# Rank products issued behind each other, and products of zeros on TensorE at the start of a two-layer mixer kernel

## The chip, the core and the metric

The kernel runs on one core of a Trainium2 chip. The metric is the device time of one launch in microseconds (us). A core has a matrix engine (TensorE, called PE in the profile, with its weight loads as PEld), a vector engine (DVE), a scalar engine (ACT), GpSimd (POOL), and queues that issue DMA transfers, above all the one of SyncE (SP). Each engine works through its own list of instructions in the order in which the program has them. An instruction that waits holds up everything behind it on its engine.

## The reference, cut to what matters

Two layers work on 256 rows of `x` and 256 rows of a context `ctx`, both 2048 wide. The change touches only the beginning of layer 0: the modulation of both inputs, and the two narrow rank columns of the first projection.

```python
sh_c, sc_c = modulation(c_c, w_ada[i], b_ada[i], 2)      # silu(cond) @ w_ada + b_ada
sh, sc, gt = modulation(c_lat, w_ada[i], b_ada[i], 3)
u  = x     * (1.0 + sc)   + sh
uc = ctx_s * (1.0 + sc_c) + sh_c
# even mixer: k, v, rf, rb, q, ... = split_cols(u @ w_in_e, E_SIZES);  rf, rb are 16 columns each
la_f = log_sigmoid(rf @ w_gate_f + b_gate_f) / 16        # decays of the linear attention, forward
la_b = log_sigmoid(rb @ w_gate_b + b_gate_b) / 16        # and backward
...
x = layer_norm(alpha * x + gt * y, ln_g[i], ln_b[i])     # then layer 1, the pooling mixer
```

## The kernel before

All matrix products against weights are made in three parts: an input and a weight are each split into a high part (`uxh`, `wh`, a cast on ACT) and a remainder (`uxl`, `wl`, a subtraction on DVE), and `mm3` (L190 to L192) adds three products of them into a PSUM bank. Weights come as raw tiles of up to 1 MB through `load_unit` (L138) on the SP queue. There are four raw buffers: a load waits until the buffer's last reader is done, which is a split on DVE for the weights that are multiplied in three parts, and PE itself for the modulation weights `w_ada` of the beginning.

The first 180 us run over the 16 blocks of 128 input columns in nine stages (`STAGES`: one block, one block, then two at a time). `stage_u` makes the inputs of a stage. `mod_rows` multiplies `silu(c)` by `w_ada` into a PSUM tile `ada` (L274): these products use 32 of the array's 128 columns, and four of them, written to four strips of 32 PSUM rows, stand side by side in the array. `to_cols` brings the sum into columns (`adaT`, L288), `x` and `ctx` are transposed (`px`, L390 and L391), and ACT and DVE make the modulated inputs `u` and their high and low parts (L393 to L401). After every fourth block come the **rank products** (L406, tile `pr`): for each of the four blocks one product of its 32 rank columns `wr` with 512 rows of input, each into its own strip of 32 rows; DVE then adds `pr` into `r_acc` (L411, L413; the tile is called `wr_acc` in the rows). There are four such groups. Between the stages, `stage_k` makes the 1024 key columns of the stage before (`kacc`, summed into `knat` by DVE, L426), and `v_fill` makes a piece of the value columns in four of the stages (`vfill`).

From 180 us on the kernel makes the rest of the value columns, the gates, the attention, the output projection, and layer 1. Beside it DVE multiplies the remaining `w_ada` weights by scalars and sums them (`aacc`, L534).

The order on each engine is not written by hand: a scheduler sets it when the program is built, from the dependencies and from a priority number that grows with the place in the source. `prio(-n)` makes the instructions inside it count as n places earlier; `issue_after` ties an instruction behind another one. PSUM tiles come from two pools of four banks each: `accp` for the sums of the three-part products, `mpp` for everything else (`ada`, `px`, `pr` and so on).

Of the kernel before, what the change touches and what calls it, by code (L numbers as in the profile page):

```python
# [2 lines left out]

# [14 lines left out]
P = 128  # L18
# [21 lines left out]
LA_LOAD = 2  # L40
FILLS = {2: [(0, 0, 2)], 4: [(0, 2, 2)], 6: [(0, 4, 2)], 8: [(0, 6, 2)]}
FILL_PRIO = 0
SPLIT_PRIO = 300
SPLIT_PRIO0 = 0
XC_PRIO = 0
# [8 lines left out]
B_X = 3000  # L54
LA_SPLIT = 1
JG = 4
STAGES = (1, 1, 2, 2, 2, 2, 2, 2, 2)


@with_exitstack  # L60
def kernel(
# [39 lines left out]
    @contextmanager  # L101
    def prio(offset):
        old = tc.cur_priority
        tc.cur_priority = max(0, old + offset)
        start = tc.cur_priority
        yield
        tc.cur_priority = old + tc.cur_priority - start

    def const(shape, dt, name):
        return cpool.tile(shape, dt, tag=name, name=name)  # L110
# [4 lines left out]
    def mp(shape, name="mp"):  # L115
        return mpp.tile(shape, F32, tag="mp", name=nm(name))
# [108 lines left out]
    nc.gpsimd.dma_start(rows2[8:24, :], as_rows(pool_scale[0]))  # L225
    nc.gpsimd.dma_start(rows2[24:26, :], as_rows(gla_norm_w[0]))

    sel4 = const([P, 4], F32, "sel4")
    nc.vector.tensor_reduce(out=sel4, in_=ident.rearrange("p (g v) -> p v g", g=4)[:, 0:4, :], axis=AX.X, op=ALU.add)

# [1 line left out]
    nc.vector.memset(sil, 0.0)  # L232
    pc = mp([P, 32], "pc")
    nc.tensor.transpose(out=pc, in_=crow, identity=ident[:32, :32])
    nc.scalar.activation(sil[:, :, 2:4], pc.rearrange("p (v k) -> p k v", v=2), AF.Silu)

    colT = const([P, 154], F32, "colT")
# [25 lines left out]
    def mod_rows(k0, n):  # L263

        nw = n * P
        ps = mp([P, nw], "ada")
        nk = 2048 // nw
        for half, c0 in ((0, D + k0 * P), (1, k0 * P)):
            for kk in range(0, KT, nk):
                r = load_unit(w_ada[0], kk, nk, c0, nw)  # L270
                for j in range(nk):
                    kt = kk + j
                    g = kt % 4
                    nc.tensor.matmul(  # L274
                        out=ps[32 * g : 32 * g + 32, :], lhsT=sil[:, kt, 2 - 2 * half : 34 - 2 * half], rhs=r[:, j, :],
                        start=half == 0 and kt < 4, stop=half == 1 and kt >= KT - 4,
                    )
        return ps

    arow_ins = []  # L280
# [85 lines left out]
    def stage_u(k0, n):  # L366
        w, n0 = n * P, k0 * P
        xc = xcs.pop(k0, None)
        if xc is None:
            xc = load_xc(k0, n)  # L370
        xs, cs = xc[:, 0:2, :], xc[:, 2:4, :]
        ps = mod_rows(k0, n)
        if k0 == 0:
            cols_0()
        if k0 == 4:
            cols_1()
        if k0 == GW_AT:
            gate_weights()
        pt = to_cols(ps, w)
        ks = slice(k0, k0 + n)  # L380
        add_bias(scT[:, ks, :], pt[:, :, 0:2], bT[0][:, 16 + k0 : 16 + k0 + n].unsqueeze(2).to_broadcast([P, n, 2]), True)
        add_bias(shT[:, ks, :], pt[:, :, 2:4], bT[0][:, ks].unsqueeze(2).to_broadcast([P, n, 2]), False)
        for j in range(n):
            kt = k0 + j
            if kt % 2 == 0:
                quad_u.append(slot([P, 2, 512], F32, "u"))
            u = quad_u[-1]
            px = mp([P, 512], "px")
            for t in range(2):
                nc.tensor.transpose(out=px[:, t * P : (t + 1) * P], in_=xs[:, t, j * P : (j + 1) * P], identity=ident)  # L390
                nc.tensor.transpose(out=px[:, 256 + t * P : 256 + (t + 1) * P], in_=cs[:, t, j * P : (j + 1) * P], identity=ident)  # L391
            ux, uc = u[:, kt % 2, 0:256], u[:, kt % 2, 256:512]
            nc.scalar.activation(ux, px[:, 0:256], AF.Identity, bias=shT[:, kt, 0:1], scale=scT[:, kt, 0:1])  # L393
            nc.vector.tensor_scalar(
                out=uc, in0=px[:, 256:512], scalar1=scT[:, kt, 1:2], scalar2=shT[:, kt, 1:2], op0=ALU.mult, op1=ALU.add
            )
            q, i = kt // 4, kt % 4
            nc.scalar.copy(uxh[q][:, i, :], ux)  # L398
            nc.scalar.copy(uch[q][:, i, :], uc)
            nc.vector.tensor_tensor(out=uxl[q][:, i, :], in0=ux, in1=uxh[q][:, i, :].bitcast(F32), op=ALU.subtract)  # L400
            nc.vector.tensor_tensor(out=ucl[q][:, i, :], in0=uc, in1=uch[q][:, i, :].bitcast(F32), op=ALU.subtract)  # L401
            if i == 3:
                pr = mp([P, 512], "pr")
                for g in range(4):
                    kk = kt - 3 + g
                    nc.tensor.matmul(  # L406
                        out=pr[32 * g : 32 * g + 32, :], lhsT=wr[:, kk, :], rhs=quad_u[kk // 2][:, kk % 2, :],
                        start=True, stop=True,
                    )
                if q == 0:  # L410
                    nc.vector.tensor_copy(r_acc, pr)  # L411
                else:
                    nc.vector.tensor_tensor(out=r_acc, in0=pr, in1=r_acc, op=ALU.add)  # L413

    def stage_k(k0, n):
        for nb in range(2):
# [971 lines left out]
```

## Time and profile before

| what | us |
|---|---|
| median of three runs | 1009.52 |
| lowest and highest of them | 1008.19, 1010.95 |
| the profiled execution, its own time | 1010.29 |
| its span from the first to the last instruction | 1008.5 |
| PE busy in the span | 960.9 (95%) |
| DVE busy in the span | 801.6 (79%) |
| ACT busy in the span | 469.3 (47%) |

The span is 1.8 us shorter than the execution's own time. A busy share is read with care on PE: matmuls are pipelined, and their ends are modelled, so that records overlap. What tells the pace of PE is the distance from one start to the next. In the chain of work that ended last, PE has 41% of the span, DVE 33% and DMA 18%.

### The profile page before, as it was taken

The numbers are of one execution on the slowest core, as the hardware profiler recorded it, in microseconds if no ns is written. First come the engines' busy times: TensorE is split into PE (matmuls) and PEld (weight loads), VectorE is DVE, ScalarE is ACT, GpSimd is POOL, SyncE is SP. The second block draws the span as 40 slices with busy tenths as digits, with TensorE's granted clock in tenths as the row PEclk, the third lists the DMA queues.
The fourth block names the chain that finished last, engine by engine and source line by source line (L and its number), as shares of the span: only waits on it lengthen the run. The fifth ranks groups of instructions, "written<-read, shape, count | busy, mean of one in ns | idle before, by whom it ended". The sixth has DMA issues, their size and how long they took to land.

```text
span 1008.5 us, 14323 instructions
## 1 busy us (share of the span) xinstructions
PE 960.9 (95%) x5654; PEld 759.2 (75%) x5654; DVE 801.6 (79%) x1142; ACT 469.3 (47%) x643; POOL 24.4 (2%) x56
## 2 busy tenths in 40 slices
PE   5899999999999999999999899999999999989995
PEld 4566656778878877887878778888778778778885
DVE  1555546979996999779999688897979997666676
ACT  2422214356675676236454344445745555435340
POOL 2000000000000000000000000000010001000000
PEclk9999999999999999999999999999999999999998
DMA  9977889566787586867767877985497999875532
GB/s 265 329 263 262 276 284 336 193 243 231 258 302 252 188 269 219 257 206 274 241 228 234 284 255 247 353 298 207 152 368 275 304 334 322 278 266 203 174 119 83
DMA packets 150371, 255.44 MB, mean 253 GB/s; under 512 B 5078, under 2 KB 46720, under 8 KB 150304
## 3 DMA queue, kind: packets, MB, share of 16 engines
q1 hardware_dynamic: 146592, 245.13, 72.4%
q0 software_dynamic: 2896, 8.72, 2.7%
q10 hardware_dynamic: 816, 0.68, 0.3%
q8 instruction: 44, 0.72, 0.3%
q14 instruction: 23, 0.19, 0.0%
HBM read 252.41 MB, written 2.10 MB: 252 GB/s over the span
## 4 chain that ended last, share of the span: by engine, by line
PE 41%; DVE 33%; DMA 18%; issue 5%; ACT 3%; SPq 0%; DVEq 0%; ACTq 0%
DMA raw<-in_w_ada_dram 15%; DVE wl L153 11%; DVE aacc L534 9%; PE oacc L191 5%; PE oacc L192 5%; PE oacc L190 5%; DMA raw<-in_w_in_o_dram 3%; PE xacc L192 3%; PE xacc L191 3%; PE xacc L190 3%; PE ada L274 2%; PE kacc L190 2%; PE kacc L192 2%; PE kacc L191 2%; PE pr L406 1%
## 5 line engine op out<-in xcount | busy, mean ns | idle before, releaser
L152 ACT CAST wh<-raw 128x1024 fp32r<-128x1024 f32 (+1 forms) x250 | 257.0, 1044 | 252.6 <-PE xacc L192 77.9
L153 DVE TENSOR_TENSOR wl<-raw,wh 128x1024 fp32r<-128x1024 f32 (+1 forms) x250 | 297.3, 1210 | 49.3 <-ACT wh L152 47.1
L534 DVE SCALAR_TENSOR_TENSOR aacc<-raw,sil,aacc 128x512 f32<-128x512 f32 x240 | 179.0, 747 | 34.2 <-DMA raw<-in_w_ada_dram 30.7
L190 PE MATMUL xacc<-wh,uxh 128*128 128x512 f32 x384 | 153.8, 400 | 0.0
L191 PE MATMUL xacc<-wl,uxh 128*128 128x512 f32 x384 | 150.9, 393 | 0.9 <-DVE wl L153 0.9
L192 PE MATMUL xacc<-wh,uxl 128*128 128x512 f32 x384 | 151.1, 394 | 0.0
L191 PEld LDWEIGHTS xacc<-wl,uxh 128*128 128x128 f32 x384 | 72.6, 189 | 17.3 <-DVE wl L153 1.7
L190 PEld LDWEIGHTS xacc<-wh,uxh 128*128 128x128 f32 x384 | 72.5, 189 | 15.6 <-issue 0.5
L192 PEld LDWEIGHTS xacc<-wh,uxl 128*128 128x128 f32 x384 | 72.4, 188 | 15.6 <-issue 0.2
L426 DVE TENSOR_TENSOR knat<-kacc,knat 128x512 f32<-128x512 f32 x64 | 42.8, 685 | 35.8 <-PE kacc L192 35.6
L285 ACT COPY arow<-ada 128x256 f32<-128x256 f32 (+1 forms) x9 | 3.1, 349 | 101.9 <-PE ada L274 101.9
L274 PE MATMUL ada<-raw,sil 128*32 128x256 f32 (+1 forms) x576 | 36.2, 380 | 12.0 <-DMA raw<-in_w_ada_dram 12.0
L190 PE MATMUL xacc<-wh,u1h 128*128 128x512 f32 x112 | 44.8, 400 | 0.8 <-ACT u1h L1167 0.8
L190 PE MATMUL oacc<-wh,y1h 128*128 128x512 f32 (+1 forms) x120 | 45.5, 379 | 0.0
L192 PE MATMUL oacc<-wh,y1l 128*128 128x512 f32 (+1 forms) x120 | 45.0, 375 | 0.0
L191 PE MATMUL oacc<-wl,y1h 128*128 128x512 f32 (+1 forms) x120 | 45.0, 375 | 0.0
L191 PE MATMUL xacc<-wl,u1h 128*128 128x512 f32 x112 | 44.1, 394 | 0.3 <-DVE wl L153 0.3
L192 PE MATMUL xacc<-wh,u1l 128*128 128x512 f32 x112 | 44.0, 393 | 0.0
L274 PEld LDWEIGHTS ada<-raw,sil 128*32 128x32 f32 x576 | 17.0, 118 | 28.6 <-issue 12.3
L190 PE MATMUL kacc<-wh,uxh 128*128 128x512 f32 x64 | 26.8, 418 | 1.5 <-ACT uxh L398 1.5
L1228 PE MATMUL xacc<-wh,dm 128*128 128x512 f32 x64 | 26.2, 409 | 1.6 <-ACT wh L152 1.6
L190 PE MATMUL kacc<-wh,uch 128*128 128x512 f32 x64 | 26.4, 412 | 0.5 <-DVE knat L426 0.5
(339 smaller groups left out, 1865.0 us busy)
## 6 DMA issues: line engine op xcount, KB each, us to landing
raw<-in_w_ada_dram SPq DMA_DIRECT2D x96, 1024.0 KB, 6.3
raw<-in_w_in_e_dram SPq DMA_DIRECT2D x54, 1024.0 KB, 6.0
raw<-in_w_in_o_dram SPq DMA_DIRECT2D x32, 1024.0 KB, 7.1
raw<-in_w_out_e_dram SPq DMA_DIRECT2D x16, 1024.0 KB, 6.7
raw<-in_w_out_o_dram SPq DMA_DIRECT2D x16, 1024.0 KB, 5.1
raw<-in_w_in_e_dram SPq DMA_DIRECT2D x18, 512.0 KB, 7.2
raw<-in_w_pool_dram SPq DMA_DIRECT2D x4, 1024.0 KB, 7.5
gt<-in_b_ada_dram POOLq DMA_DIRECT2D x8, 256.0 KB, 3.8
```

Source lines behind the costliest of these rows:

```text
L152: nc.scalar.copy(h, r[:, j : j + w, :])
L153: nc.vector.tensor_tensor(out=l, in0=r[:, j : j + w, :], in1=h.bitcast(F32), op=ALU.subtract)
L190: nc.tensor.matmul(out=acc, lhsT=uh, rhs=wh, start=start, stop=False)
L191: nc.tensor.matmul(out=acc, lhsT=uh, rhs=wl, start=False, stop=False)
L192: nc.tensor.matmul(out=acc, lhsT=ul, rhs=wh, start=False, stop=stop)
L274: nc.tensor.matmul(out=ps[32 * g : 32 * g + 32, :], lhsT=sil[:, kt, 2 - 2 * half : 34 - 2 * half], rhs=r[:, j, :], start=half == 0 and kt ...
L285: arow_ins.append(nc.scalar.copy(a[:, :nw], ps))
L406: nc.tensor.matmul(out=pr[32 * g : 32 * g + 32, :], lhsT=wr[:, kk, :], rhs=quad_u[kk // 2][:, kk % 2, :], start=True, stop=True,)
L426: nc.vector.tensor_tensor(out=dst, in0=acc, in1=dst, op=ALU.add)
L534: e.scalar_tensor_tensor(out=a, in0=r[j], scalar=sc, in1=a, op0=ALU.mult, op1=ALU.add)
L1228: nc.tensor.matmul(out=accs[0], lhsT=dh, rhs=wh, start=f, stop=False)
```

## The change

Two things are done. First, a constant tile `zero` is cleared by DVE, and `keep_warm` issues full-precision products of zeros, 128x128 by 128x256, into a PSUM tile `idle` that nobody reads: seven behind the first transpose, six behind the products of the first raw tile of `w_ada`, two behind the four transposes of the first block. Second, the rank products move into a function `ranks`. The product of the group's last block is issued first, and the other three are tied behind it; all four stand in a `prio(-PR_PRIO)` of 200 places. The sum that they form is the same.

```diff
+PR_PRIO = 200
+WARM = (7, 6, 2)
+    zero = const([P, 256], F32, "zero")
+    nc.vector.memset(zero, 0.0)
+
+    def keep_warm(n, behind=None):
+        idle = mp([P, 256], "idle")
+        for _ in range(n):
+            with tc.issue_after(behind.ins) if behind else nullcontext():
+                nc.tensor.matmul(out=idle, lhsT=zero[:, 0:P], rhs=zero, start=True, stop=True)
...
     nc.tensor.transpose(out=pc, in_=crow, identity=ident[:32, :32])
+    keep_warm(WARM[0])
...
+            if k0 == 0 and half == 0:
+                keep_warm(WARM[1], ins)
...
+            if kt == 0:
+                keep_warm(WARM[2], ins)
...
             if i == 3:
-                pr = mp([P, 512], "pr")
-                for g in range(4):
-                    kk = kt - 3 + g
-                    nc.tensor.matmul(
-                        out=pr[32 * g : 32 * g + 32, :], lhsT=wr[:, kk, :], rhs=quad_u[kk // 2][:, kk % 2, :],
-                        start=True, stop=True,
-                    )
...
+                ranks(kt)
+
+    def ranks(kt):
+
+        pr = mp([P, 512], "pr")
+
+        def product(g):
+            kk = kt - 3 + g
+            return nc.tensor.matmul(
+                out=pr[32 * g : 32 * g + 32, :], lhsT=wr[:, kk, :], rhs=quad_u[kk // 2][:, kk % 2, :], start=True, stop=True)
+
+        with prio(-PR_PRIO):
+            first = product(3)
+            with tc.issue_after(first.ins):
+                for g in range(3):
+                    product(g)
```

At the start of PE's list, before (`pc` are small transposes, `xc` the two inputs as loaded; a row with x16 stands for sixteen products):

```order
L234 MATMUL pc_108<-ident,crow_87 128x32
L274 MATMUL ada_140<-raw_141,sil 32x128 x16
L274 MATMUL ada_140<-raw_159,sil 32x128 x16
L247 MATMUL pc_1_177<-ident,rows_1_84 128x32
L288 MATMUL adaT_182<-sel_104,arow_180 128x4
L390 MATMUL px_187<-ident,xc_91 128x128
...
L391 MATMUL px_187<-ident,xc_91 128x128
L190 MATMUL kacc_267<-wh_200,uxh_116 128x512
```

The same place in the changed program:

```order
L246 MATMUL pc_110<-ident,crow_87 128x32
L238 MATMUL idle_112<-zero 128x256 x7
L287 MATMUL ada_150<-raw_151,sil 32x128 x16
L238 MATMUL idle_169<-zero 128x256 x6
L287 MATMUL ada_150<-raw_176,sil 32x128 x16
...
L406 MATMUL px_204<-ident,xc_91 128x128
L238 MATMUL idle_209<-zero 128x256 x2
L287 MATMUL ada_233<-raw_234,sil 32x128 x16
L192 MATMUL kacc_287<-wh_220,uxh_126 128x512
```

The zeros stand where PE had nothing to do before, and the third block of modulation products (raw_214 before, raw_234 now) has moved ahead of the first key product.

On PE at the second rank group, before, behind the transposes `px` of the eighth block:

```order
L391 MATMUL px_749<-ident,xc_686 128x128
L406 MATMUL pr_760<-u_549,wr_acc_113 32x512 x2
L190 MATMUL kacc_798<-wh_682,uxh_120 128x512
L191 MATMUL kacc_798<-wl_683,uxh_120 128x512
L406 MATMUL pr_760<-u_737,wr_acc_113 32x512
L192 MATMUL kacc_798<-wh_682,uxl_121 128x512
L190 MATMUL kacc_798<-wh_682,uxh_120 128x512
L406 MATMUL pr_760<-u_737,wr_acc_113 32x512
L191 MATMUL kacc_798<-wl_683,uxh_120 128x512
```

The same group in the changed program, behind seventeen key products:

```order
L194 MATMUL kacc_834<-wh_702,ucl_133 128x512
L192 MATMUL kacc_834<-wh_702,uch_132 128x512
L428 MATMUL pr_780<-u_757,wr_acc_123 32x512
L428 MATMUL pr_780<-u_569,wr_acc_123 32x512 x2
L428 MATMUL pr_780<-u_757,wr_acc_123 32x512
L193 MATMUL kacc_834<-wl_703,uch_132 128x512
L194 MATMUL kacc_834<-wh_702,ucl_133 128x512
```

Three separate interruptions of the key products became one. The other groups look the same: three interruptions in the third group, two in the first and the last before, one in each now.

On DVE in the same stage the split `swl` of the value weights moved ahead. Before:

```order
L413 TENSOR_TENSOR wr_acc_113<-pr_760,wr_acc_113 128x512
L426 TENSOR_TENSOR knat_132<-kacc_798,knat_132 128x512
L426 TENSOR_TENSOR knat_133<-kacc_806,knat_133 128x512
L153 TENSOR_TENSOR swl_833<-raw_830,swh_832 128x1024
L426 TENSOR_TENSOR knat_134<-kacc_814,knat_134 128x512
```

Now:

```order
L155 TENSOR_TENSOR swl_853<-raw_850,swh_852 128x1024
...
L452 TENSOR_TENSOR knat_142<-kacc_818,knat_142 128x512
L452 TENSOR_TENSOR knat_143<-kacc_826,knat_143 128x512
L418 TENSOR_TENSOR ucl_133<-u_757,uch_132 128x256
L439 TENSOR_TENSOR wr_acc_123<-pr_780,wr_acc_123 128x512
L452 TENSOR_TENSOR knat_144<-kacc_834,knat_144 128x512
```

The split now stands ahead of the sums of the key products, and the addition of the rank sum behind two of them.

## Rows read from the trace of the kernel before

**Rows 1.** Windows by stage: busy us of PE, PEld, DVE, ACT, POOL; clock, DMA, GB/s.
```profile
0.00:40.00 40.00, 26.55 (x254) 18.12 (x254) 11.90 (x29) 10.92 (x22) 7.04 (x17) 1.00 1.05 298
40.00:180.00 140.00, 136.61 (x880) 88.89 (x873) 81.21 (x139) 40.66 (x74) 0.41 (x2) 1.00 0.87 282
180.00:300.00 120.00, 118.03 (x541) 96.52 (x541) 111.90 (x170) 69.75 (x105) 0.71 (x7) 1.00 0.72 247
```

**Rows 2.** Timeline of PE, first 26 us: start, duration, work [idle before, releaser].
```profile
7.67 1.93 PE L274 MATMUL ada<-raw,sil 128*32 128x128 f32 x32 [4.86 <-DMA raw<-in_w_ada_dram]
12.14 1.94 PE L274 MATMUL ada<-raw,sil 128*32 128x128 f32 x32 [2.54 <-DMA raw<-in_w_ada_dram]
17.09 0.80 PE L190 MATMUL kacc<-wh,uxh 128*128 128x512 f32 x1 [1.09 <-ACT uxh L398]
...
18.11 0.63 PE L190 MATMUL kacc<-wh,uxh 128*128 128x512 f32 x1
18.54 0.63 PE L191 MATMUL kacc<-wl,uxh 128*128 128x512 f32 x1
...
20.81 1.50 PE L274 MATMUL ada<-raw,sil 128*32 128x128 f32 x32
...
23.27 0.39 PE L190 MATMUL kacc<-wh,uxh 128*128 128x512 f32 x1
23.50 0.39 PE L191 MATMUL kacc<-wl,uxh 128*128 128x512 f32 x1
...
24.27 1.08 PE L274 MATMUL ada<-raw,sil 128*32 128x128 f32 x32
```

**Rows 3.** Timeline of the SP queue, two of its loads.
```profile
9.65 4.86 SPq L138 DMA_DIRECT2D raw<-in_w_ada_dram  x2
14.57 4.06 SPq L211 DMA_DIRECT2D xc<-in_x_dram  x1
```

**Rows 4.** Windows of 5 us, columns as in rows 1.
```profile
15.00:20.00 5.00, 3.91 (x12) 2.93 (x12) 2.73 (x7) 2.18 (x5) 0.00 (x0) 1.00 1.13 236
30.00:35.00 5.00, 5.00 (x34) 3.36 (x33) 4.34 (x9) 0.00 (x0) 0.00 (x0) 1.00 1.09 348
```

**Rows 5.** The chain that ended last, one piece: start, duration, what.
```profile
31.10 8.15 DMA raw<-in_w_ada_dram
```

**Rows 6.** Timeline around the first rank group, PE and ACT.
```profile
39.30 1.07 PE L274 MATMUL ada<-raw,sil 128*32 128x256 f32 x16 [1.84 <-DMA raw<-in_w_ada_dram]
...
42.33 1.92 PE L406 MATMUL pr<-u,wr_acc 128*32 128x512 f32 x6
42.47 1.03 ACT L152 CAST swh<-raw 128x1024 fp32r<-128x1024 f32 x1
...
44.18 0.73 PE L190 MATMUL vfill<-swh,uxh 128*128 128x512 f32 x2
```

**Rows 7.** Timeline of PE in the second rank group.
```profile
86.72 1.05 PE L406 MATMUL pr<-u,wr_acc 128*32 128x512 f32 x4
...
88.36 1.04 PE L406 MATMUL pr<-u,wr_acc 128*32 128x512 f32 x2
89.34 0.50 PE L192 MATMUL kacc<-wh,uxl 128*128 128x512 f32 x1
89.67 0.40 PE L190 MATMUL kacc<-wh,uxh 128*128 128x512 f32 x1
90.00 1.05 PE L406 MATMUL pr<-u,wr_acc 128*32 128x512 f32 x2
```

**Rows 8.** Timelines of PE and of DVE at the last rank group.
```profile
172.59 1.92 PE L406 MATMUL pr<-u,wr_acc 128*32 128x512 f32 x6
...
175.10 1.04 PE L406 MATMUL pr<-u,wr_acc 128*32 128x512 f32 x2
...
176.18 0.69 DVE L413 TENSOR_TENSOR wr_acc<-pr,wr_acc 128x512 f32<-128x512 f32 x1 [1.91 <-PE pr L406]
```

**Rows 9.** Timeline of PE: modulation blocks that wait, first and last of three.
```profile
105.11 1.07 PE L274 MATMUL ada<-raw,sil 128*32 128x256 f32 x16 [0.82 <-DMA raw<-in_w_ada_dram]
...
166.16 1.07 PE L274 MATMUL ada<-raw,sil 128*32 128x256 f32 x16 [0.74 <-DMA raw<-in_w_ada_dram]
```

**Rows 10.** Waits over the span: us in total, times, longest.
```profile
DVE aacc L534 <- DMA raw<-in_w_ada_dram: 30.7, 12, 5.6
```

More of the change, by code (lines that the diff above doesn't have):

```diff
@@ L1 @@
 import math
-from contextlib import ExitStack, contextmanager
+from contextlib import ExitStack, contextmanager, nullcontext
 import concourse.bass as bass
@@ L273, in mod_rows @@
                     g = kt % 4
-                    nc.tensor.matmul(
+                    ins = nc.tensor.matmul(
                         out=ps[32 * g : 32 * g + 32, :], lhsT=sil[:, kt, 2 - 2 * half : 34 - 2 * half], rhs=r[:, j, :],
@@ L390, in stage_u @@
                 nc.tensor.transpose(out=px[:, t * P : (t + 1) * P], in_=xs[:, t, j * P : (j + 1) * P], identity=ident)
-                nc.tensor.transpose(out=px[:, 256 + t * P : 256 + (t + 1) * P], in_=cs[:, t, j * P : (j + 1) * P], identity=ident)
+                ins = nc.tensor.transpose(out=px[:, 256 + t * P : 256 + (t + 1) * P], in_=cs[:, t, j * P : (j + 1) * P], identity=ident)
+            if kt == 0:
+                keep_warm(WARM[2], ins)
             ux, uc = u[:, kt % 2, 0:256], u[:, kt % 2, 256:512]
@@ L402, in stage_u @@
             if i == 3:
-                pr = mp([P, 512], "pr")
-                for g in range(4):
-                    kk = kt - 3 + g
-                    nc.tensor.matmul(
-                        out=pr[32 * g : 32 * g + 32, :], lhsT=wr[:, kk, :], rhs=quad_u[kk // 2][:, kk % 2, :],
-                        start=True, stop=True,
-                    )
[L410 to L413, printed above, removed]
+                ranks(kt)
[10 more added lines that the diff above has]
+                    product(g)
+        if kt == 3:
+            nc.vector.tensor_copy(r_acc, pr)
+        else:
+            nc.vector.tensor_tensor(out=r_acc, in0=pr, in1=r_acc, op=ALU.add)
     def stage_k(k0, n):
```

## The prediction

> **What bounds the kernel now.** I read the windows by stage first, then the timeline of PE through the stages that the change touches, then the queue that feeds them. From 40 to 180 us PE is busy 136.6 of 140 us, DVE 81.2 and ACT 40.7 [rows 1]: PE sets the pace there, and an interval taken off its list shortens the stage. Up to 40 us PE is busy only 26.6 us, while DMA moves 298 GB/s [rows 1]. There the transfers bind: the rate is 348 GB/s in the window from 30 us, and the chain waits 8.15 us from the issue of a modulation load at 31.10 us to its landing at 39.3 us [rows 4, 5], where PE has stood idle for 1.84 us [rows 6]. From 180 to 300 us DVE is busy 111.9 of 120 us beside PE's 118.0 [rows 1]; both are full, so that stage neither adds nor takes away time if it simply starts earlier.
>
> **The start: zeros.** The profile grants clock 1.00 throughout [rows 1], but the same work runs at two rates. A block of 16 modulation products takes 1.93 and 1.94 us at 7.67 and 12.14 us, 1.50 us at 20.81 us and 1.08 us at 24.27 us; key products start 0.43 us apart at 18.11 us and 0.23 us apart at 23.27 us [rows 2]. [...]
>
> A product of zeros is not in this trace. The block is its nearest row: 16 products of 128 columns, four side by side, are four rounds of 128 columns, as long as two full products of 256. So one product of zeros costs about 1.94 / 2 = 0.97 us at the low level and 1.08 / 2 = 0.54 us at the high one (estimates from these rows). Seven cost 6.8 or 3.8 us, six 5.8 or 3.2 us, two 1.9 or 1.1 us.
>
> The seven start where PE falls idle, 7.67 - 4.86 = 2.81 us [rows 2], and end at 6.6 us if they run high and at 9.6 us if they run low; the first raw tile lands at 7.67 us. The six follow the first block, and the second tile lands at 12.14 us. If everything runs high, the second block goes from 12.14 to 13.2 us, and its raw buffer is free 0.9 us earlier than now (14.1 us). If everything runs low, the first block starts at 9.6 and ends at 11.5 us, the six end at 17.3 us, and the second block ends at 19.3 us, 5.2 us late. In between, with the rise during the seven, the first block ends near where it does now, the six run high, and the second block ends between 13.2 and 13.9 us. I take 0.8 us earlier, near the end where everything runs high: the seven leave PE no pause, as the stretch from 17.09 us did. The two zeros behind the transposes lie in the 1.09 us that PE waits for `uxh` [rows 2], and so cost nothing at the high level.
>
> From there the products up to 22 us run at the high level: about nine key products at 0.43 - 0.23 us and a block at 1.50 - 1.08 us make 2.2 us, and with the 0.9 us this is 3.1 us. That is the upper end, and I don't take it, because at 39.3 us PE waits for a load. What the loads gain is what the second block's buffer gains: the queue holds the next load until that block is done (the pair of loads from 9.65 us ends at 14.5 us), and the load of `xc` stands behind it for 4.06 us [rows 3]. The slack of the transfers is in the window from 15 us, 236 GB/s against 348 [rows 4]: 5 x (348 - 236) / 348 = 1.6 us. So the start is worth **0.8 us** of time, with -5.2 and +3.1 as its ends. The `zero` tile costs one clearing on DVE before DVE has other work. The three `idle` tiles take banks of a pool of four, but each is done before a bank is asked for again.
>
> **The rank groups.** One product of a group has two records in the trace. Two products side by side took 1.05 us at 86.72 us, and one alone took 1.04 us at 88.36 us [rows 7]: a lone product pays for the whole pass. The eight products of 256 columns in a modulation block at 105.11 us take 1.07 us [rows 9]; in four strips they are two rounds of 256 columns, the same length as one round of 512. So four rank products behind each other should take about 1.05 us. An interruption also pushes the key products apart: from 88.36 us it is 0.98 us to the next key product, and then 0.33 us instead of 0.23 us to the one after [rows 7], in all 1.08 us.
>
> In the second group three interruptions become one: 2 x 1.08 = **2.2 us**, with the key products already there to fill PE. The third group has the same pattern: **2.2 us**. In the last one, 1.92 us and 1.04 us [rows 8] become 1.05 us: **1.9 us**. The first group is different. Its 1.92 us at 42.33 us run while ACT makes `swh`, which is done at 42.47 + 1.03 = 43.5 us and which the value products at 44.18 us need [rows 6]. In the new order the rank products stand behind ten value products, so that this cover is gone: PE waits to 43.5 us, the value products start 0.6 us earlier, and the rank group costs 1.05 us later instead of 1.04 us. That leaves **0.6 us**; if the weights come earlier it is up to 1.9 us.
>
> [...]
>
> **What moves with it.** The new lists put several modulation blocks ahead of key products. At 105.11, 128 and 166.16 us these blocks already wait for their tile, 0.82 us at the first and 0.74 us at the last [rows 9], and key products that stood ahead of them now stand behind. Against that, DVE splits earlier in the second group (`swl` ahead of the key sums), which frees the raw buffer and issues the load earlier. I set the two against each other at zero, with -4.4 us as the lower end (below). At the last group DVE stands 1.91 us waiting for `pr`, with the next splits behind it [rows 8]; the new order has three sums and splits ahead of that addition, and up to 1.9 us more could come from it. I take nothing, since PE is full there.
>
> **Sum.** 0.8 + 0.6 + 2.2 + 2.2 + 1.9 = 7.7 us. Nothing later is tied to a fixed time: the loads wait for buffers, and buffers for PE and DVE, so I let all of it reach the end. Against the profiled execution, 1010.3 us, this gives 1002.6 us. The median of the runs, 1009.5 us, lies 0.8 us lower, and a result will be a median as well: **1001.8 us**.
>
> **Rivals.** (a) The zeros keep PE from the modulation tiles without raising the clock. This needs the low level through all thirteen; it loses 5.2 us at the start, with the transfers bound behind it, and the rank groups give 6.9: 1009.5 + 5.2 - 6.9 = 1007.8 us. For it speaks that the level stayed low through both modulation blocks; against it, that those had pauses of 4.86 and 2.54 us ahead of them [rows 2].
>
> (b) The rank gain turns into waits for modulation tiles. In five stages two to five key products now stand behind such a block, about 19 in all, at 0.23 us each 4.4 us; if the loads come no earlier, PE idles that long. 1001.8 + 4.4 = 1006.2 us. For it: three blocks wait today [rows 9]. Against it: the earlier splits.
>
> (c) Slower: DVE takes over behind 180 us. There the scheduler has also moved sums `aacc` of modulation weights ahead of splits and of key sums. DVE waits 30.7 us for such tiles in all today, 5.6 us at most at once [rows 10]; whatever stands behind such a wait, splits above all, holds PE. If these waits grow by more than the 7.7 us gained, the kernel is slower. With waits half as long again (15 us) it would take 1001.8 + 15 = 1016.8 us. Against it: the new places are a few instructions from the old ones, and both the tile and DVE come earlier together.
>
> **How the numbers follow.** The forecast has 0.66, (a) 0.08, (b) 0.18, (c) 0.08. About 0.3% or 3 us is what a measurement of this kernel can tell from no change, so that faster is below 1006.5 us. The forecast and two thirds of (b) are faster: 0.66 + 0.12 = 0.78. Case (a) and the rest of (b) are the same: 0.14. Case (c) is slower: 0.08. The range reaches from 1001.8 - 4.3, where the start gives 3.1 us, the first group 1.9 us and DVE's wait some of its 1.9 us, to 1008 us, which takes in (b) and (a): 997.5 to 1008 us.
>
> **What would show it.** The blocks on the first two tiles should take 1.1 us, at least the second one. The wait that ends at 39.3 us should end near 38.5 us and still be for a modulation tile. The four groups should stand as blocks of eight records of about 1.05 us. The last group's time should come about 7 to 8 us earlier than 175 us, and the distance should hold to the end. I would be wrong on the start if the second block ended later than 14.1 us; on the groups if four products together took much more than 1.1 us; on the rest if PE's waits for modulation tiles between 50 and 180 us grew by some microseconds, or if the distance won at 180 us were smaller at 300 us.

## The result and the profile after

The changed kernel takes **998.11 us** (median of four runs, 996.14 to 1001.09) where the kernel before takes 1008.86 us beside it: a ratio of 0.9896, 95% interval 0.9862 to 0.9929, so 10.7 us or 1.0% less. Two later sets of runs gave 995.41 us (0.9886, 0.9853 to 0.9919) and 995.50 us (0.9875, 0.9845 to 0.9905). The forecast was 1001.8 us, a gain of 7.7 us, with 997.5 to 1008 us as its range; the two later medians lie below it. The sign and the mechanism of the groups hold; the gain is larger, and it is made up otherwise than the sum said. Ratios here and below leave out three executions that took 1367 to 3059 us, one of a variant and two of the kernel before.

The profiled execution took 1001.09 us, the longest of the four, with a span of 999.3 us. Its windows by stage, columns as in [rows 1]:

```profile
0.00:40.00 40.00, 31.35 (x268) 22.61 (x268) 12.42 (x30) 10.84 (x22) 7.04 (x17) 0.96 1.03 291
40.00:180.00 140.00, 136.83 (x915) 96.41 (x916) 86.10 (x146) 42.05 (x75) 0.41 (x2) 0.96 0.92 298
180.00:300.00 120.00, 118.55 (x549) 97.47 (x548) 113.55 (x173) 74.17 (x112) 1.92 (x10) 1.00 0.72 249
```

PE is still busy almost all the time from 40 to 180 us. The clock is new: 0.96 in the first two of these windows, where [rows 1] had 1.00. The timeline of PE in the first 26 us (start, duration, engine, line, work, records, idle time before) says where:

```profile
2.83 5.13 PE L238 MATMUL idle<-zero 128*128 128x256 f32 x14
7.89 1.08 PE L287 MATMUL ada<-raw,sil 128*32 128x128 f32 x32
8.90 2.86 PE L238 MATMUL idle<-zero 128*128 128x256 f32 x12
11.98 1.08 PE L287 MATMUL ada<-raw,sil 128*32 128x128 f32 x32 [0.22 <-DMA raw<-in_w_ada_dram]
...
14.16 1.03 PE L238 MATMUL idle<-zero 128*128 128x256 f32 x4
18.99 1.08 PE L287 MATMUL ada<-raw,sil 128*32 128x128 f32 x32 [3.80 <-DMA raw<-in_w_ada_dram]
...
20.83 0.63 PE L194 MATMUL kacc<-wh,uxl 128*128 128x512 f32 x1
21.25 0.63 PE L192 MATMUL kacc<-wh,uxh 128*128 128x512 f32 x1
```

The seven zeros take 5.13 us, and the pace rises inside them: windows of 0.5 us touch two or three of their records from 3.3 to 6.8 us and four from 6.8 to 7.8 us, and both modulation blocks take 1.08 us instead of 1.93 and 1.94 us [rows 2]. But the third block now stands ahead of all key products, and PE waits 3.80 us for its tile. The block itself still takes 1.08 us, but the key products behind it start 0.43 us apart, and the clock granted is 0.50 from 20.5 to 23.5 us. This pace is the low level of the prediction, that of [rows 2] at 18.11 us; the high one is 0.23 us, as at 25.42 us here. The SP queue is ahead of [rows 3] by 1.0 us (the load of `xc` issued at 13.55 instead of 14.57 us), and yet 5 us windows show the same traffic at 15 us as [rows 4]:

```profile
15.00:20.00 5.00, 1.20 (x34) 0.85 (x33) 1.51 (x4) 0.77 (x2) 0.00 (x0) 1.00 1.13 243
20.00:25.00 5.00, 5.00 (x46) 3.73 (x42) 0.00 (x0) 1.76 (x3) 0.00 (x0) 0.66 1.04 298
30.00:35.00 5.00, 4.93 (x34) 3.53 (x33) 4.26 (x7) 0.34 (x1) 0.00 (x0) 1.00 1.10 351
```

Around the first rank group (answers to [rows 6]) PE waits for a tile, for `arow` and for `swh`, the clock granted is 0.50 from 41 to 51 us, and the value products stand 0.43 us apart until 51 us:

```profile
40.65 1.91 PE L287 MATMUL ada<-raw,sil 128*32 128x256 f32 x16 [1.93 <-DMA raw<-in_w_ada_dram]
43.04 1.02 PE L303 MATMUL adaT<-sel,arow 128*128 128x4 f32 x4 [0.48 <-ACT arow L300]
...
46.60 1.22 PE L192 MATMUL vfill<-swh,uxh 128*128 128x512 f32 x2 [0.73 <-ACT swh L154]
...
49.32 0.63 PE L192 MATMUL vfill<-swh,uxh 128*128 128x512 f32 x1
49.75 0.63 PE L193 MATMUL vfill<-swl,uxh 128*128 128x512 f32 x1
...
51.10 1.06 PE L428 MATMUL pr<-u,wr_acc 128*32 128x512 f32 x8
```

The second and the last group (answers to [rows 7, 8]) stand as one block each, eight records in 1.07 and 1.06 us (timeline of PE; the third, at 134.50 us, in 1.07 us), and DVE takes the last one without a wait (timeline of DVE):

```profile
93.34 0.39 PE L192 MATMUL kacc<-wh,uch 128*128 128x512 f32 x1
93.66 1.07 PE L428 MATMUL pr<-u,wr_acc 128*32 128x512 f32 x8
94.66 0.50 PE L193 MATMUL kacc<-wl,uch 128*128 128x512 f32 x1
...
173.79 1.06 PE L428 MATMUL pr<-u,wr_acc 128*32 128x512 f32 x8
```

```profile
175.77 0.68 DVE L439 TENSOR_TENSOR wr_acc<-pr,wr_acc 128x512 f32<-128x512 f32 x1
```

**Where the time went.** The kernels order their work differently, so that one tile is no mark. I counted the 3456 products of 512 columns (rank products aside) in each timeline and compared when the 140th, the 600th and the 3000th start (75, 230 and 875 us in the kernel before). One product more or less on either side of a mark is 0.23 us. The part from the 140th to the 600th holds the second, the third and the last group. In us against the profile of before:

| kernel | 140th | 600th | 140th to 600th | 3000th |
|---|---|---|---|---|
| forecast | -1.4 | -7.7 | -6.3 | -7.7 |
| changed | +3.3 | -8.1 | -11.4 | -8.9 |
| changed, again | +0.6 | -9.6 | -10.2 | -12.2 |
| changed, third | +0.2 | -10.4 | -10.6 | -11.5 |
| before, again | +0.2 | 0.0 | -0.2 | -0.2 |

So the part up to 75 us lost where a gain was forecast, and the part with the second, third and last group gave 10.2 to 11.4 us instead of 6.3. Behind 230 us an execution wins or loses some microseconds more; that is treated below.

### The profile page after: what moved, and what is told of

The parts are those of the page before. It is cut to its first block, busy times and chain, and to the rows that moved or that the text cites. A ratio compares the mean times of both kernels' runs of the same rounds, so it can differ in the third digit from the quotient of the medians.

```text
span 999.3 us, 14376 instructions
## 1 busy us (share of the span) xinstructions
PE 959.7 (96%) x5684; PEld 767.0 (77%) x5684; DVE 801.0 (80%) x1143; ACT 469.4 (47%) x643; POOL 24.4 (2%) x56
## 4 chain that ended last, share of the span: by engine, by line
PE 56%; DVE 24%; DMA 14%; issue 3%; ACT 2%; SPq 1%; DVEq 0%; ACTq 0%
DMA raw<-in_w_ada_dram 11%; DVE wl L155 8%; PE oacc L193 6%; PE oacc L192 6%; PE oacc L194 6%; DVE aacc L560 6%; PE xacc L194 6%; PE xacc L192 6%; PE xacc L193 6%; DMA raw<-in_w_in_o_dram 3%; PE kacc L192 2%; PE ada L287 2%; PE kacc L193 2%; PE kacc L194 2%; ACT wh L154 1%
## 5 line engine op out<-in xcount | busy, mean ns | idle before, releaser
L560 DVE SCALAR_TENSOR_TENSOR aacc<-raw,sil,aacc 128x512 f32<-128x512 f32 x240 | 178.8, 747 | 31.2 <-DMA raw<-in_w_ada_dram 27.8
L192 PE MATMUL oacc<-wh,y1h 128*128 128x512 f32 (+1 forms) x120 | 45.5, 379 | 0.0
L287 PE MATMUL ada<-raw,sil 128*32 128x256 f32 (+1 forms) x576 | 33.9, 367 | 7.8 <-DMA raw<-in_w_ada_dram 7.7
L193 PE MATMUL kacc<-wl,uxh 128*128 128x512 f32 x64 | 26.0, 407 | 0.0
```

What stands on the lines that cost most here:

```text
L192: nc.tensor.matmul(out=acc, lhsT=uh, rhs=wh, start=start, stop=False)
L193: nc.tensor.matmul(out=acc, lhsT=uh, rhs=wl, start=False, stop=False)
L287: ins = nc.tensor.matmul(out=ps[32 * g : 32 * g + 32, :], lhsT=sil[:, kt, 2 - 2 * half : 34 - 2 * half], rhs=r[:, j, :], start=half == 0 a ...
L560: e.scalar_tensor_tensor(out=a, in0=r[j], scalar=sc, in1=a, op0=ALU.mult, op1=ALU.add)
```

## The experiments

**The change split in two.** Two theories stood against each other. G: the groups carry the gain, the zeros give nothing or cost a little. Z: the zeros give the start its gain as a rule, and the profiled execution was unlucky. Four kernels ran on one chip: the changed kernel again, the groups alone, the zeros alone, and the groups with seven zeros. Stages are counted from zero here and in what was expected: the first two have one block each, so that the second stage is the first with two. Its `adaT` products, which turn a finished modulation sum into columns, serve as its mark; the kernel before has them at 40.87 us.

```diff
 after_again: the changed kernel as it is
 rank_only:
-    keep_warm(WARM[0])
-            if k0 == 0 and half == 0:
-                keep_warm(WARM[1], ins)
-            if kt == 0:
-                keep_warm(WARM[2], ins)
 zeros_only:
-                ranks(kt)
+                (the loop over g and the addition of the kernel before)
 seven_zeros:
-WARM = (7, 6, 2)
+WARM = (7, 0, 0)
```

> The changed kernel once more, unaltered. Theory G (the groups carry the gain; the zeros give nothing or cost a little): about 998 us, and the profile shows again that PE waits about 3.8 us for the third modulation block and that the second stage's adaT products come at about 43 us, some 2 us later than in the kernel before (40.87 us), because the clock has fallen. Theory Z (the zeros give the start its forecast gain as a rule, and the profiled execution was an unlucky one): the time is about the same, but a second profile has these adaT products at 40 us or earlier.

> The rank groups alone, without any product of zeros; it computes the same. Theory G: all of the gain stays, 997 to 999 us, and the start up to 45 us is that of the kernel before (adaT of the second stage at 40.9 us). Theory Z: by the sum of the prediction the groups alone give 6.9 us against the kernel before, so about 1002 us, 3 to 4 us behind the changed kernel.

> The three sets of zeros alone, with the rank products where the kernel before has them; it computes the same. Theory G: 1008 to 1011 us, the second stage's adaT products at about 43 us, that is 2 us late, as in the profile of the changed kernel. Theory Z: 1004 to 1006 us, with these products before 40.9 us.

> The rank groups with the seven zeros ahead of the first modulation block, without the six and the two. PE's order is then that of the groups alone: key products stand ahead of the third modulation block, which the six zeros had pushed behind it. Theory G, with the reorder as what the start loses: no wait of 3.8 us at 19 us, clock high from 8 us on in the first block, adaT of the second stage at or before 40.9 us, and the time equal to the groups alone within 1.5 us. Theory Z: without the six, the second block is at the low level again (1.9 us), and the time is 2 to 3 us above the changed kernel.

| kernel | median | ratio to before, interval | 140th | 600th | 140th to 600th | 3000th |
|---|---|---|---|---|---|---|
| changed, again | 995.41 | 0.9886 (0.9853 to 0.9919) | +0.6 | -9.6 | -10.2 | -12.2 |
| groups alone | 997.73 | 0.9911 (0.9881 to 0.9942) | +0.8 | -9.0 | -9.8 | -13.3 |
| zeros alone | 1006.30 | 0.9993 (0.9969 to 1.0018) | +0.5 | -1.1 | -1.7 | -2.0 |
| groups, seven zeros | 999.59 | 0.9929 (0.9904 to 0.9954) | +1.7 | -9.0 | -10.7 | -7.7 |

The groups alone keep the gain; the zeros alone can't be told from no change. G holds on the time of the groups, with three misses. The second stage's `adaT` products were at 40.81 us in the repeat, not at 43 us. With seven zeros they were at 41.73 us, not at 40.9 us or before (the time is 1.9 us above the groups alone, where 1.5 was the bound). With the zeros alone they were at 41.35 us, not at 43 us, and the time was 1006.30 us, below G's 1008 to 1011 us. Timeline of PE behind the third block, in the repeat, and then the start of the kernel with seven zeros:

```profile
18.95 1.08 PE L287 MATMUL ada<-raw,sil 128*32 128x128 f32 x32 [3.71 <-DMA raw<-in_w_ada_dram]
19.97 0.50 PE L192 MATMUL kacc<-wh,uxh 128*128 128x512 f32 x1
20.30 0.40 PE L193 MATMUL kacc<-wl,uxh 128*128 128x512 f32 x1
20.54 0.40 PE L194 MATMUL kacc<-wh,uxl 128*128 128x512 f32 x1
```

```profile
12.09 1.08 PE L289 MATMUL ada<-raw,sil 128*32 128x128 f32 x32 [2.42 <-DMA raw<-in_w_ada_dram]
...
19.11 1.08 PE L289 MATMUL ada<-raw,sil 128*32 128x128 f32 x32 [1.45 <-DMA raw<-in_w_ada_dram]
```

After 3.71 us of waiting the clock stayed high here (1.00 from 15 to 25 us, key products 0.24 us apart); in the first profile it fell to 0.50 behind a wait of 3.80 us. In the kernel with the first group apart, which follows below, the block takes 1.93 us after only 3.17 us:

```profile
19.06 1.93 PE L287 MATMUL ada<-raw,sil 128*32 128x128 f32 x32 [3.17 <-DMA raw<-in_w_ada_dram]
```

With seven zeros the order is that of the groups alone, the blocks take 1.08 us at 12.09 and 19.11 us and 1.07 us at 36.12 us, and still the third block waits 1.45 us for its tile, which lands at 19.1 us. In six of the nine profiles in which PE comes there early the block starts at 18.95 to 19.11 us, in the other three at 19.92 to 20.50 us. This is what the traces show of why the zeros earn so little: with the blocks at 1.08 us PE only waits longer for the same transfers, 3.71 and 3.80 us ahead of the third block in these two profiles of the changed kernel.

**The first group.** In all three profiles of the changed kernel, in that of the groups alone and in that with seven zeros the clock is low between 40 and 50 us; in the two of the kernel before and in that of the zeros alone it is not. From 40 to 45 and from 45 to 50 us it is 0.57 and 0.50, 0.61 and 0.71, 0.92 and 0.74 in those of the changed kernel, 0.60 and 0.71 with the groups alone, and 1.00 in the first one of before; with seven zeros transposes stand 0.21 us apart there, and 0.11 us in the second one of before and with the zeros alone. Theory C put the low clock on the rank products that no longer fill PE's wait for `swh`.

```diff
 first_apart (first_apart_nz: the same on rank_only):
-        with prio(-PR_PRIO):
+        if kt == 3:
+            for g in range(4):
+                product(g)
+        else:
             first = product(3)
 first_zeros:
-            if kt == 0:
-                keep_warm(WARM[2], ins)
+            if kt in (0, 3):
+                keep_warm(WARM[2] if kt == 0 else 4, ins)
```

> The changed kernel with its first rank group put back as it was: three products ahead of the value products, the fourth behind ten of them; the other three groups stay together. Theory C (the first group lost its cover: PE now stands idle for the split of the value weights, its clock falls to the low level there, and the work up to 85 us pays for it): no granted clock below 1 between 40 and 50 us, 22.6 us from the second stage's adaT products to the third's instead of 23.2 to 23.7, 44.5 us to the fourth's instead of 45.3 to 46.1, and the end 1 to 1.5 us earlier than the changed kernel, about 994 us. Rival (the 0.5 us wait for arow and the wait for the load ahead of it make the clock fall, whatever stands behind): the clock falls all the same, and the time is that of the changed kernel plus 0.9 us for one more pass.

> As the one before, but without any product of zeros. Theory C and the theory that the zeros are worth nothing: within 1.5 us of the one before, and 1 to 2 us earlier than the groups alone. If the zeros carry a part of the gain, it is 2 us or more behind the one before.

> The changed kernel with four more products of zeros behind the transposes of the second stage's second tile, where PE waits for the split of the value weights; the first rank group stays together. By theory C the zeros keep the clock as the three rank products did: granted clock 1 between 40 and 50 us, adaT to adaT about 22.5 us, and the four zeros (2.1 us at the high level) cost what they last beyond the wait of 0.73 us, about 1.4 us, so that the end is within 1 us of the changed kernel. By the rival the clock falls all the same and the kernel is 1.5 to 3 us slower than the changed one.

| kernel | median | ratio, interval | 140th | 600th | 140th to 600th | 3000th |
|---|---|---|---|---|---|---|
| first group apart | 1001.73 | 0.9918 (0.9891 to 0.9945) | +0.3 | -8.7 | -8.9 | -9.7 |
| the same, no zeros | 1000.23 | 0.9920 (0.9894 to 0.9945) | +0.8 | -7.6 | -8.5 | -9.7 |
| four zeros more | 997.61 | 0.9884 (0.9852 to 0.9915) | 0.0 | -9.4 | -9.4 | -7.9 |

C explains a part only. With the first group apart the clock held between 40 and 50 us (1.00), but without zeros it fell all the same (0.66 from 40 to 45 us). And in most profiles it falls too early for C. The rows show the groups alone, whose order is that of the kernel before up to here; transposes `px` 0.21 us apart are at the low level (0.11 us in the kernel before):

```profile
39.53 1.07 PE L286 MATMUL ada<-raw,sil 128*32 128x256 f32 x16 [1.84 <-DMA raw<-in_w_ada_dram]
41.09 1.02 PE L300 MATMUL adaT<-sel,arow 128*128 128x4 f32 x4 [0.49 <-ACT arow L297]
...
42.21 0.42 PE L403 MATMUL px<-ident,xc 128*128 128x128 f32 x1
42.43 0.42 PE L402 MATMUL px<-ident,xc 128*128 128x128 f32 x1
```

The waits of 1.84 and 0.49 us are those of the kernel before ([rows 6] show the first), ahead of the place where the orders part; one of 0.62 us for a tile at 36.62 us is new. The 13 profiles fall into two sets. In five the clock fell ahead of the transposes, and PE had waited 1.84 to 2.12 us for the tile of the block ahead of them. In eight the transposes were fast, and this wait had been 0.58 to 1.84 us. Among these eight C's pattern holds: with the group together it fell at the wait for `swh` in both (1.15 us each, and 0.74 granted from 45 to 50 us; the third profile of the changed kernel and that with second passes, below), with the group apart or as before it held in four, and with four more zeros in two. What makes the clock fall at these waits in one execution and not in another stays open; what it costs doesn't. From the second stage's `adaT` products to the fourth's it is 44.48 us in the kernel before (44.49 in its second profile). With the first group together it is 45.3 to 46.1 us in the four profiles where the clock fell ahead of the transposes (the longest has a wait of 1.22 us for a tile besides), 44.25 and 44.77 us in the two where it fell at `swh`, and 43.24 us with four more zeros, where the clock held (42.90 us in the kernel with late zeros below, which has the same four):

```profile
43.39 1.89 PE L238 MATMUL idle<-zero 128*128 128x256 f32 x8
44.93 0.81 PE L192 MATMUL vfill<-swh,uxh 128*128 128x512 f32 x2
...
47.32 1.07 PE L428 MATMUL pr<-u,wr_acc 128*32 128x512 f32 x8
```

So this stretch is 1.2 to 1.6 us shorter with the clock held, and 0.8 to 0.9 us longer when the clock falls early (the longest left aside).

None of the three variants beats the changed kernel. Behind 75 us the two with the group apart are no test of the first group alone: their edit takes `prio(-PR_PRIO)` from the other three groups too, which stay together but lose their 200 places. Between the fourth and the eighth stage's `adaT` products their modulation products stand in 12 or 13 separate blocks, as in the kernel before (12 and 13), and in 9 or 10 where the first group is together. Its key products take 45.0 and 45.3 us there (before 45.5 us; 183 products each), those of the changed kernel 43.6 to 43.7 us (181 products, of which the difference in number makes 0.5 us). Whether the first group or the lost priority brings the old blocks back was not tested. But the stretch shows what standing together gives without these blocks moved: 80.01 and 80.66 us, against 85.87 us before and 77.9 to 78.9 us in the changed kernel and the groups alone.

**The later waits.** Behind 380 us PE has three long waits, 5.14, 1.55 and 3.59 us in the kernel before (581, 747 and 889 us), 2.96, 2.66 and 3.22 us in the changed one (571, 738 and 880 us). The clock falls there in most profiles, and not in the same ones in all. In these two it falls at all three: 0.83 from 580, from 745 and from 885 us (10 us each) before, 0.77 from 565 to 580 us and 0.83 from 735 and from 875 us (10 us each) in the changed kernel. Theory D: this is what differs from execution to execution. To test it, five zeros were set ahead of each.

```diff
 late_zeros (first_zeros, and):
+        if hp == 1:
+            keep_warm(5)              # ahead of the last yT
...
+                if n0 == 512 and kt == 0:
+                    keep_warm(5, end[0])   # end[0]: last product of the block before
...
+        if g == 2:
+            keep_warm(5)              # ahead of the third y1T
```

> The kernel with four zeros in the first group (first_zeros) and five more products of zeros at each of three later waits of PE: ahead of the transposes of the last y (about 567 us, PE idle 2.6 to 3.8 us in the profiles so far), ahead of the second block of differences (735 us, 1.2 to 3.0 us) and ahead of the third transposes of the gate (876 us, 2.2 to 3.5 us). Theory D (what differs behind 380 us from execution to execution is the clock falling at these waits, 1 to 3 us each time): no window below 0.95 between 560 and 600, 735 and 750, 875 and 890 us, 3 to 4 us earlier than the changed kernel, 992 to 994 us, and the runs lie closer together than 4 us. Rival (the waits themselves, which end with DVE or ACT, set the pace, and the low level behind them is hidden by the next wait, or five zeros of 2.6 us run past a short wait): the time of the changed kernel within 1 us, whatever the clock shows.

> The changed kernel beside it on the same chip: 0.989 of the kernel before. In its profile a clock below 1 near 570, 735 or 880 us wherever the time is over 996 us; by theory D the difference to the kernel with late zeros is the sum of these windows' losses.

Late zeros: 998.11 us, 0.9897 (0.9871 to 0.9923). The changed kernel beside it: 995.50 us, 0.9875 (0.9845 to 0.9905). Windows of the kernel with late zeros, and from its timeline of PE what is left of two of the waits:

```profile
560.00:600.00 40.00, 38.94 (x184) 32.22 (x185) 32.47 (x54) 19.11 (x23) 0.72 (x1) 1.00 0.87 306
730.00:750.00 20.00, 18.94 (x85) 14.85 (x85) 14.98 (x17) 11.84 (x14) 1.08 (x2) 1.00 1.04 374
775.00:785.00 10.00, 7.11 (x29) 5.91 (x30) 8.90 (x12) 4.83 (x6) 1.06 (x2) 0.83 0.89 279
```

```profile
569.03 0.74 PE L1002 MATMUL yT<-ident,y 128*128 128x128 f32 x4 [1.06 <-DVE y L992]
...
879.46 1.09 PE L1321 MATMUL y1T<-ident,gate 128*128 128x128 f32 x8 [1.65 <-DVE gate L1368]
```

The clock is 1.00 at all three places (from 875 to 890 us too). That the zeros hold it is not shown: it is 1.00 at all three in the first repeat of the changed kernel as well, while it fell at two or three of them in its other profiles. The transposes start no earlier than without them (569.03 us; 567.67 and 568.17 us in the repeats of the changed kernel), the clock falls at another wait (0.83 from 775 us), and the time is not better: 2.6 us longer in the median, where D had 992 to 994 us and its rival a difference within 1 us. D falls as a lever: where DVE or ACT ends a wait, no effect of the clock behind it is shown here.

**Does PE's time still reach the end?** Three groups were given a second pass each.

```diff
-                for g in range(3):
+                for g in (0, 1, 2) if kt == 3 else (0, 1, 2, 3, 0, 1, 2):
                     product(g)
```

> The changed kernel with the four products of the second, third and last group issued twice (the second time writes the same values again): one more pass in each of three groups, some 0.9 us each by the 1.92 us that six records took before. It tells whether an interval of PE in these stages still reaches the end once the groups stand together. Theory P (PE sets the pace from 85 to 180 us, and what it saves or loses there goes through to the end): 1.8 us later at 171 us, 2.7 us later at 380 us and at the end, that is 0.992 of the kernel before instead of 0.989. Rival (the loads of the modulation tiles already set the pace there, since PE waits 1.3 to 1.9 us for them in the changed kernel): PE's waits for them between 85 and 171 us shrink by about as much, to under 0.5 us, and the end is within 1 us of the changed kernel.

Measured: 1001.04 us, 0.9928 (0.9900 to 0.9956), 3 to 5 us above the changed kernel's 0.9896, 0.9886 and 0.9875 (the intervals overlap). A second pass adds 0.86 us to the 1.06 (timeline of PE):

```profile
91.63 1.92 PE L428 MATMUL pr<-u,wr_acc 128*32 128x512 f32 x16
```

From the 140th to the 600th product it wins 6.7 us instead of 10.2 to 11.4: at least 3.5 us gone for 2.6 us of passes. The eighth stage's `adaT` products come no later (164.85 us), but with 172 key products since the fourth stage's instead of 181. P holds: PE's intervals go through. By the rival the waits for modulation tiles between 85 and 171 us should have shrunk; they rose to 2.9 us (1.3 to 1.9 us in the changed kernel's profiles).

## Why the prediction was right, and where not

**Bound by PE from 40 to 180 us: right behind 85 us**, shown by the kernel with second passes; ahead of that it was not tested. **Nothing lost behind it: right.** The 8.1 to 10.4 us of the 600th product are 8.9 to 12.2 us at the 3000th.

**The start, 0.8 us: mis-sized, and its step on the loads was wrong.** The rise came inside the seven zeros (5.13 us, between the 3.8 and 6.8 us of the two levels), as it had come behind the products from 17.09 us, inside the block of 1.50 us at 20.81 us [rows 2], on which the choice of 0.8 us rested; that work without a pause brings it was my reading of that place and is not shown as a rule. The six ran high (2.86 us), the second block ended at 13.1 us (13.2 to 13.9 us were named), and the buffer came 1 us earlier. But "slack of the transfers, 1.6 us" was none: the window from 15 us went from 236 only to 243 GB/s, and the wait at 39.3 us ended at 39.25 us in the repeat and at 40.65 us in the first profile, not at 38.5 us. I had also looked only at what the zeros cost on PE, not at what they do to the scheduler's order: the six and the two, which the kernel with seven zeros lacks, push the third block ahead of all key products, and at the wait of 3.2 to 5.3 us there the clock fell in some profiles (3.17, 3.78 and 3.80 us) and held in another (3.71 us).

**The first group, 0.6 us: the wrong sign in most profiles.** The step itself (cover gone, 0.73 us of wait, one pass instead of three) came as written. What it left out is the clock, which the sum took as high behind 22 us and which was 0.50 from 41 to 51 us in the first profile. With four more zeros, where the clock held (1.00 from 40 to 50 us), the stretch is 1.2 us shorter.

**The second, third and last group, 6.3 us: too small, 9.8 to 11.4 us measured.** Four products take 1.06 to 1.07 us, a lone one 1.04 us [rows 7], as forecast: 1.02 to 1.03 times one product. I summed the rows of PE's timeline between the fourth and the eighth stage's `adaT` products, before against the groups alone: 85.87 to 77.91 us, for two of the groups, which the forecast had at 4.4 us. Of these 7.96 us the rank products give 3.88 (5.88 to 2.00), the key products 1.92 (45.51 for 183 to 43.59 for 181, so 0.46 of it for two products outside the marks), the transposes 0.34, and the waits for tiles 1.96, less 0.15 for the blocks. The 2.2 us for a group had 1.08 us for an interruption; the key product ahead of it (0.33 us to the next start instead of 0.23 us, the one at 89.67 us in [rows 7]) and the transposes ahead were forgotten, and that modulation blocks would stand together was not seen as a gain. And the waits that I set at zero with -4.4 us as the lower end fell. PE's waits for modulation tiles from 85 to 171 us (us in all, times, longest) are in the kernel before

```profile
PE ada L274 <- DMA raw<-in_w_ada_dram: 2.8, 3, 1.2
```

in the changed kernel

```profile
PE ada L287 <- DMA raw<-in_w_ada_dram: 1.3, 2, 1.0
```

and in the groups alone

```profile
PE ada L286 <- DMA raw<-in_w_ada_dram: 0.8, 2, 0.5
```

How much of this fall is the groups' own is open. The repeats of the changed kernel have 1.9 and 1.7 us of such waits, the second profile of the kernel before has 2.6 us, and the zeros alone, with rank products as before, have 2.0 us and win 1.7 us from the 140th to the 600th product.

**The last group's place as a sign: not met.** It stands at 173.79 us, 1.3 us ahead of 175.10 us and not 7 to 8 us, because the new order has put it behind key products; the count of products shows the gain that this tile does not.

**The 1.9 us of DVE that I took as nothing came in part.** From the eighth stage's `adaT` products (171 us) to 380 us the changed kernel is 3.2, 4.1 and 3.5 us shorter in its three profiles, 1.8 us of it from the rank products (2.81 to 1.00). Of PE's waits there those for DVE's `rp` and `knat` are gone, 0.8 and 0.5 us (0.5 and 0.5 us in the second profile of the kernel before). The list of these waits of the kernel before, and behind it that of the changed one:

```profile
PE nT L685 <- ACT qn L792: 1.1, 1, 1.1
PE xacc L191 <- DVE wl L153: 0.9, 2, 0.7
PE pz L723 <- DVE rp L707: 0.8, 1, 0.8
PE kacc L190 <- DVE knat L426: 0.5, 1, 0.5
```

```profile
PE nT L711 <- ACT qn L818: 1.1, 1, 1.1
PE xacc L193 <- DVE wl L155: 0.9, 2, 0.6
```

**The rivals.** (a) fell with the first rows of the timeline: the blocks took 1.08 us. It had a point all the same, that zeros can earn nothing. (b) fell: the waits went down, not up. (c) fell: DVE's waits for modulation tiles, 30.7 us before [rows 10], are 27.8 us in the changed kernel. So two errors of opposite sign met: about 2 to 5 us too much for the part up to 75 us, 4 to 5 us too little for the groups behind it. That the total lay inside the range was in part luck.

**Open.** Behind 230 us profiles differ by some microseconds with the same order of work. From the 600th to the 3000th product the three profiles of the changed kernel won 0.8, 2.6 and 1.1 us; the groups alone won 4.2 us there, and the groups with seven zeros lost 1.2 us. The second profile of the kernel before, taken to see what differs by itself, is within 0.2 us of the first at both marks. Whether 1 or 2 us of the gain there belong to the change is not settled. Nor is it whether the zeros are worth 2.5 us beside the groups: 0.9886 and 0.9911 have intervals that overlap, and with the first group apart the kernels with and without zeros are level (0.9918 and 0.9920).

## What to carry to other kernels

Narrow products between full ones cost a pass each here (0.98 us), plus a slower neighbour on both sides (0.33 instead of 0.23 us): put those that share a pass behind each other, and count the neighbours, the transposes and the blocks that move together with them. Work that was only to keep the clock up earned nothing that could be told here (zeros alone: 0.9993, 0.9969 to 1.0018), where a transfer ended the waits, and it moved real work in the scheduler's order; look at the order first. When a variant is meant to undo one part of a change, see that its edit leaves the rest as it was. With orders that differ, compare two traces at equal work done, not at one tile, and take a second profile of the kernel before to see what differs by itself.

## What the hardware showed that was not expected

- In these profiles the clock's fall does not follow from the length of the wait alone. Behind 3.17 us (first group apart) and 3.78 us (zeros alone) the third modulation block took 1.93 and 1.94 us, the low level; behind 3.80 us it took 1.08 us and the key products after it stood 0.43 us apart; behind 3.71 us it took 1.08 us and they stood 0.24 us apart. At waits of 1.84 and 0.49 us the clock fell in the groups alone (transposes 0.21 us apart), with one of 0.62 us ahead of them, and held in the kernel before (0.11 us).
- The profile grants clock 1.00 in the first 20 us of the kernel before, where key products stand 0.43 us apart; behind the zeros and blocks of 1.08 us, the profile of the changed kernel shows the later fall as 0.66 (20 to 25 us; 0.50 from 20.5 to 23.5 us). The low level of the start showed in the spacing of products only.
- From start to next start a lone pass of rank products takes 0.98 to 1.00 us and two behind each other 1.85 us, so that a lone pass is some 0.15 us dearer than one that follows its like.
